# Turned tiles' transfers on SyncE, both far heads scaled by VectorE, and casts placed behind the weights' casts

## The chip, the cores and the metric

The kernel runs on one core of a Trainium2 chip. Its engines are TensorE (PE, matrix products), VectorE (DVE), ScalarE (ACT), GpSimd (POOL) and SyncE (SP, which here only issues transfers). The metric is device microseconds of one execution: 1052.34 us before the change, the median of 3 runs (1051.72 to 1052.66).

## What is computed

One layer of a hybrid encoder over 512 tokens of width 1024, in float32. From the normalised input h one combined projection feeds four mixers, whose outputs are gated and merged; a cross-attention into 256 memory tokens and a gated MLP follow. The change touches the two attentions among the mixers, and the preparation of the memory tokens:

```
# differential attention: 4 heads, two score maps each, chunk-causal
p = softmax(where(mask, q_c k_c^T * scale, -inf))       # c = 0, 1
out = (p[0] - lam * p[1]) v
# forgetting attention: 8 heads, frame-causal
c = cumsum(log_sigmoid(f_g + b_fgt))
s = q k^T * scale + c_q - c_k
out = softmax(where(mask, s, -inf)) v
# memory tokens, for the cross-attention
m = rms_norm(mem) ;  xk, xv = split(m @ w_xkv)
```

## The kernel before

**Precision.** Every operand of a large product is split into a high part (a cast to TensorE's fast float32) and a low part (the rest). A product takes three matmuls: high by high, high by low, low by high (`mm3`, L235 to L244).

**Weights.** A weight block of 512 KB is loaded by SP (`load_raw`, L164; the transfer's own line is L176) into one of two buffers `wr`. ACT casts it to `wh` (L192), then DVE subtracts for `wl` (L193). There are four buffers of each. `run_blocks` (L206) prepares blocks three jobs ahead of the one whose matmuls run. `last_weights` (L179) holds the last block's cast and subtraction.

**Background tasks.** Between the blocks, `Background` (L47) gives steps to generators: the attention of a head or of a pair of heads, and the memory tokens. A step has a planned cost and a wait before the next one. So the attention's small operations lie between weight blocks on every engine. The program then goes through a scheduler, which reorders the instructions of each engine by planned times. An edit of one instruction's engine therefore changes the order of others. `tc.issue_after(x)` holds an instruction behind instruction x in that order.

**PSUM.** Four kinds of tiles have two banks each: `ps_mm` (projections), `ps_av` (values), `ps_sc` (scores), `ps_tr` (transposes). A matmul into a bank waits until the reader of the tile that was there before is done. Readers of `ps_mm` are, by stage: ACT's copy and DVE's subtraction of a values block (`split`, L155 and L156), the same for queries and keys (L806 to L818), the tanh of a gate block on ACT (L1165), and DVE's merge of a branch (L1177). Readers of `ps_sc` are DVE's evacuations L929 (differential) and L1123 (forgetting), which add a mask or a bias and take a maximum.

**Attention.** `a_task` (L896) handles one head of the differential attention, `f_task` (L1055) a pair of heads of the forgetting attention. For each of the four query tiles of 128 rows (width w = 128 to 512 keys) the scores are made, evacuated, exponentiated on ACT (L934, L1129) and scaled. Then the probabilities must be turned, so that keys lie on partitions. There are two ways. *Near* heads (h = 3, and pairs 2 and 3) use TensorE's transposes (`to_keys_major`, L830). *Far* heads (h < 3, and pairs 0 and 1) turn squares of 32 by 32 on DVE (`turn_squares`, L845, recorded at L848), write the tile to DRAM (`put`, L850), read it back in another order into `ptl` (`get`, L859), then cast it in place on ACT to `pth` (L867) and subtract on DVE (L868). `values` multiplies these with v.

**Who issues, before.** `put` is issued by ACT. `get` is issued by ACT in `f_task`, held behind the last evacuation that `main` (L840) has noted, and by POOL in `a_task`. The casts of `split_in_place` (L863) are held behind that same noted evacuation. `mem_task` (L1291) turns two memory tiles in the same way, with its put on ACT and its get on POOL. In `f_task` each pair's first head is scaled by ACT (L1136) and the second by DVE (L1134). `GETS` and `SPLITS` (L893) say at which step a far head's tiles are read back and cast.

Of the kernel before, what the change touches and what calls it, by code (L numbers as in the profile page):

```python
# [17 lines left out]
F32 = mybir.dt.float32  # L18
# [7 lines left out]
P = 128  # L26
# [57 lines left out]
def hybrid_layer(ctx: ExitStack, tc: tile.TileContext, a: dict, out: bass.AP):  # L84
    nc = tc.nc
    V, A, G, PE, SP = nc.vector, nc.scalar, nc.gpsimd, nc.tensor, nc.sync
# [44 lines left out]
    for i in range(8):  # L131
        n = ("wh", "wl")[i % 2]
# [3 lines left out]
        elif i < 6:  # L136
            n = ("fz_raw", "fz", "fe", "fu", "fd")[i - 1]
# [41 lines left out]
    last_weights = []  # L179
# [200 lines left out]
    for i, plan in enumerate(plans):  # L380
        r_t = m1p.tile([P, P], F32, tag="fbias" if i == 2 else "ck", name=f"rows{i}", bufs=2)
        n = 0
# [19 lines left out]
    for t in range(2):  # L402
        y_t = m1p.tile([P, D], F32, tag="ptl", name="nt", bufs=2)
# [95 lines left out]
    for i in range(2):  # L499
        for p in range(3):  # L500
            first_half(i, p, w_g[i], glu[2:])
            if p == 2 - i:
                with tc.issue_after(casts[-1].ins):
                    y_t = normed(m1p, xs[:, 2 + i], gain, m1p.tile([P, D], F32, tag="ptl", name="nt", bufs=2), late)
# [345 lines left out]
    def put(e, w):  # L850
        d = dram.tile([2, P * S], F32, tag="turned", name="turned", bufs=6)[:e.shape[1], :P * w]
        d = d.rearrange("h (p x) -> p h x", p=P)
        A.dma_start(d, e[:, :, :w])
        return d

    def part_of(pt, n, local):
        return pt[:, local, :, :n].rearrange("p a t i -> p a (t i)")

    def get(d, n, pt, local, queue=A):  # L859
        with tc.issue_after(evacuations[0]) if queue is A else ExitStack():  # L860
            queue.dma_start(part_of(pt[1], n, local).bitcast(F32), d.rearrange("(a j) (b x) -> (j b) a x", j=32, b=4))  # L861

    def split_in_place(n, pt, local):  # L863
        hi, lo = (part_of(x, n, local) for x in pt)
        raw = lo.bitcast(F32)
        with tc.issue_after(evacuations[0]):
            A.copy(hi, raw)  # L867
        V.tensor_tensor(lo, raw, hi.bitcast(F32), ALU.subtract)  # L868

# [26 lines left out]
    def a_task(h, qk, v):  # L896
        es, pt, av = {}, None, None
        far = h < 3
        yield 0.0, 3.0
        for step in range(8 if far else 6):  # L900
            if step in ((5, 7) if far else (3, 5)):
                if av is None:
                    av = bank("av")
                vh, vl = (x[:, :, h * P:(h + 1) * P] for x in v[0])
                with tc.issue_after(steps_of[0]) if far else ExitStack():
                    values(av, lambda kt: ((vh[:, kt], 0), (vh[:, kt], 1), (vl[:, kt], 0)), pt,
                           step // 2 - (2 if far else 1))
            cost = 0.0
            if far:
                for qt in SPLITS.get(step, ()):  # L910
                    split_in_place(qt + 1, pt, qt % 2)
                    cost += 0.1 + 0.15 * qt
                for qt in GETS.get(step, ()):
                    if qt % 2 == 0:
                        pt = pt_tiles()
                    get(es.pop(qt)[:, 0], qt + 1, pt, qt % 2, G)
            elif 1 <= step <= 4:
                if step in (1, 3):
                    pt = pt_tiles()
                to_keys_major(es.pop(step - 1)[:, 0], step, pt, (step - 1) % 2)  # L920
                cost += 0.1 + 0.15 * step
            if step < 4:
                qt, w = step, (step + 1) * P
                e = es[qt] = e4()
                st = m1p.tile([P, 8], F32, tag="st8", name="st8", bufs=4)
                for c in range(2):
                    ps = bank("sc")
                    scores(ps, qk, c, qt * P, w)
                    V.tensor_tensor_reduce(e[:, c, :w], ps[:, :w], mask_a[:, S - w:], scale=1.0,  # L929
                                           scalar=-3.0e38, op0=ALU.add, op1=ALU.max,  # L930
                                           accum_out=st[:, c:c + 1])
                V.tensor_scalar(st[:, 2:4], st[:, 0:2], -HD ** -0.5, None, ALU.mult)
                for c in range(2):
                    A.activation(e[:, c, :w], e[:, c, :w], AF.Exp, bias=st[:, 2 + c:3 + c],  # L934
                                 scale=HD ** -0.5, accum_out=st[:, 4 + c:5 + c])
                V.reciprocal(st[:, 6:8], st[:, 4:6])
                V.tensor_scalar(st[:, 7:8], st[:, 7:8], lam, None, ALU.mult)
                A.activation(e[:, 1, :w], e[:, 1, :w], AF.Copy, scale=st[:, 7:8])
                V.scalar_tensor_tensor(e[:, 0, :w], e[:, 0, :w], st[:, 6:7], e[:, 1, :w], ALU.mult,
                                       ALU.subtract)  # L940
                cost += 0.6 + 0.0035 * w
                if far:
                    turn_squares(e[:, 1, :w], e[:, 0, :w])
                    es[qt] = put(e[:, 1:], w)
                    cost += 0.0015 * w
            if step == (7 if far else 5):
                e = e4()
                A.copy(e[:, 0], av)
            yield cost, (6.0 if step == 5 else 4.0) if far else 3.5

        ps = bank("tr")
        for t in range(NT):
            transpose(ps[:, t * P:(t + 1) * P], e[:, 0, t * P:(t + 1) * P])
        A.activation(e[:, 1], ps, AF.Square, scale=1.0 / math.sqrt(P))
        ms = m1p.tile([P, NT], F32, tag="ms4", name="ms4", bufs=2)
        V.tensor_reduce(ms, e[:, 1].rearrange("p (t c) -> p t c", t=NT), AX.X, ALU.add)
        r = rstd_of(m1p, [ms], NT)
        V.tensor_tensor(e[:, 0].rearrange("p (t c) -> p t c", t=NT),
                        ps.rearrange("p (t c) -> p t c", t=NT),
                        r.unsqueeze(2).to_broadcast([P, NT, P]), ALU.mult)  # L960
        yield 1.5, 3.5
        ps2 = bank("tr")
        for t in range(NT):
            transpose(ps2[:, t * P:(t + 1) * P], e[:, 0, t * P:(t + 1) * P])
        if "a" not in y:
            y["a"] = (y8b(), y8b())
        split(ps2, y["a"][0][:, h], y["a"][1][:, h], half["dn"])
        yield 0.6, 0.0
# [86 lines left out]
    def f_task(p, qk, v):  # L1055
# [19 lines left out]
        for step in range(8 if far else 6):  # L1075
# [33 lines left out]
            if step < 4:  # L1109
                qt, w = step, (step + 1) * P  # L1110
                e = es[qt] = e4()
                st = m1p.tile([P, 8], F32, tag="st8", name="st8", bufs=4)
                for j in range(2):
                    head = 2 * p + j
                    bias = m1p.tile([P, S], F32, tag="fbias", name="fbias", bufs=2)

                    G.tensor_scalar(bias[:, :w], ck[j][:, :w], -1.0, cq[:, qt, head:head + 1],  # L1117
                                    ALU.mult, ALU.add)
                    G.affine_select(out=bias[:, w - P:w], in_=bias[:, w - P:w], pattern=[[-1, P]],
                                    compare_op=ALU.is_ge, fill=BIG, base=0, channel_multiplier=1)  # L1120
                    ps = bank("sc")
                    scores(ps, qk, j, qt * P, w)
                    V.tensor_tensor_reduce(e[:, j, :w], ps[:, :w], bias[:, :w], scale=1.0,  # L1123
                                           scalar=-3.0e38, op0=ALU.add, op1=ALU.max,
                                           accum_out=st[:, j:j + 1])
                V.tensor_scalar(st[:, 2:4], st[:, 0:2], -HD ** -0.5, None, ALU.mult)
                turn_ready()
                for j in range(2):
                    A.activation(e[:, j, :w], e[:, j, :w], AF.Exp, bias=st[:, 2 + j:3 + j],  # L1129
                                 scale=HD ** -0.5, accum_out=st[:, 4 + j:5 + j])  # L1130
                V.reciprocal(st[:, 6:8], st[:, 4:6])
                for j in range(2):
                    if j:
                        V.tensor_scalar(e[:, j, :w], e[:, j, :w], st[:, 6 + j:7 + j], None, ALU.mult)  # L1134
                    else:
                        A.activation(e[:, j, :w], e[:, j, :w], AF.Copy, scale=st[:, 6 + j:7 + j])  # L1136
                cost += 0.6 + 0.0038 * w
                if far:
                    ready.append((qt, e, w))
                    cost += 0.003 * w  # L1140
# [150 lines left out]
    def mem_task():  # L1291
        for t in range(2):
# [8 lines left out]
                             y_t[:, i * S:(i + 1) * S])  # L1301
                yield 1.0, 0.0
            d = dram.tile([P * D], F32, tag="turned_m", name="turned_m", bufs=2)
            A.dma_start(d.rearrange("(p x) -> p x", p=P), m_t)
            G.dma_start(y_t.rearrange("p (a x) -> p a x", a=4), d.rearrange("(a j b x) -> (j b) a x", a=4, j=32, b=4))
            yield 0.0, 18.0
            hi, lo = (x[:, :, t * P:(t + 1) * P].rearrange("p k (a i) -> p k a i", a=4) for x in ns.mt)
            raw = y_t.rearrange("p (a k i) -> p k a i", a=4, i=32)
# [583 lines left out]
```

## Time and profile before

| | |
|---|---|
| median of 3 runs | 1052.34 us (1051.72 to 1052.66) |
| the profiled execution | 1052.56 us |
| its span in the trace | 1050.8 us, 14439 instructions |
| granted TensorE clock | 0.998 |
| DVE subtractions for `wl` (L193) | 140, 174.2 us |
| DMA | 163.85 MB, mean 156 GB/s |
| transfers issued on SP's queue | 38.0% of 16 engines' span |
| on ACT's queue | 8.9% |
| on POOL's queue | 3.7% |

A page of the profile shows one execution. Its first part gives busy time per engine, the second cuts the span into 40 slices of some 26 us and gives each engine's busy share in tenths (9 means 90% or more). Group lines read: line, engine, operation, output<-inputs by the program's names, shapes, count, total busy time, mean ns of one, and then the idle time of the engine just before them with what ended it. Timeline lines read: start, duration, engine, line, operation, and in brackets the idle time before it and its releaser. Lines that begin ACTq, POOLq or SPq are the issue of a transfer. Releasers are inferred.

### The profile page before, as it was taken

Reading aid. Unit: us, or ns where it says so; the run is one execution under the profiler, and the core shown is the slowest. Engines: PE = TensorE matmul, PEld = TensorE weight load, DVE = VectorE, ACT = ScalarE, POOL = GpSimd, SP = SyncE. Lnnn points to the kernel's source line nnn. Section 1 sums busy time; section 2 is a strip of 40 time slices with the busy share of each in tenths; the row PEclk is TensorE's granted clock in tenths of the full one; section 3 lists DMA queues with packets and bytes.
Section 4 is the critical chain, followed back from the end, with each engine's and each line's share of the span. In section 5 each row is a group of like instructions: output and inputs, shape, how many; then the busy total and the mean of one; then the engine's idle time right before and its main releaser. Section 6 shows DMA issues by size and latency. Waiting matters only on the chain.

```text
span 1050.8 us, 14439 instructions
## 1 busy us (share of the span) xinstructions
PE 1039.2 (99%) x5255; PEld 883.0 (84%) x5255; DVE 807.2 (77%) x1265; ACT 508.9 (48%) x838; POOL 157.7 (15%) x253
## 2 busy tenths in 40 slices
PE   9999999999999999999999999999999999999997
PEld 8888888888888988788888899999888888888886
DVE  7899998687777458776577898776767777667796
ACT  5322222376566355665434665655343333445662
POOL 4001000101210114422111031121112111111001
PEclk9999999999999999999999999999999999999999
DMA  7954333324433245652346834235676666725672
GB/s 249 316 164 104 103 99 100 101 83 124 134 104 111 60 120 172 182 149 82 100 154 230 277 121 124 78 101 182 194 246 221 220 223 219 220 81 181 214 216 80
DMA packets 175708, 163.85 MB, mean 156 GB/s; under 512 B 12543, under 2 KB 146924, under 8 KB 175637
## 3 DMA queue, kind: packets, MB, share of 16 engines
q1 hardware_dynamic: 152995, 119.91, 38.0%
q10 hardware_dynamic: 19122, 31.47, 8.9%
q0 software_dynamic: 3520, 11.56, 3.7%
q8 instruction: 41, 0.67, 0.3%
q14 instruction: 30, 0.25, 0.1%
HBM read 139.43 MB, written 23.48 MB: 155 GB/s over the span
## 4 chain that ended last, share of the span: by engine, by line
PE 90%; issue 4%; DVE 2%; ACT 1%; DMA 1%; POOL 1%; ACTq 0%; POOLq 0%; DVEq 0%
PE ps_mm L235 47%; PE ps_av L235 29%; PE ps_sc L235 7%; PE ps_tr L235 4%; PE ps_tr L241 2%; DMA ptl<-turned 1%; PE ps_mm L453 1%; PE ps_av L453 1%; POOL fbias L1117 0%; DMA xs<-in_x 0%; DVE qk L808 0%; ACT wh L192 0%; ACTq L861 0%; DVE e L1123 0%; DVE wl L193 0%
## 5 line engine op out<-in xcount | busy, mean ns | idle before, releaser
L192 ACT CAST wh<-wr 128x1024 fp32r<-128x1024 f32 (+1 forms) x140 | 146.7, 1048 | 258.9 <-PE ps_mm L235 156.9
L193 DVE TENSOR_TENSOR wl<-wr,wh 128x1024 fp32r<-128x1024 f32 (+1 forms) x140 | 174.2, 1245 | 86.3 <-ACT wh L192 86.0
L235 PE MATMUL ps_mm<-hth,wh 128*128 128x512 f32 (+1 forms) x616 | 230.8, 381 | 1.0 <-ACT wh L192 0.7
L235 PE MATMUL ps_mm<-hth,wl 128*128 128x512 f32 (+1 forms) x616 | 229.9, 379 | 0.0
L235 PE MATMUL ps_mm<-htl,wh 128*128 128x512 f32 (+1 forms) x616 | 229.8, 379 | 0.0
L235 PEld LDWEIGHTS ps_mm<-hth,wh 128*128 128x128 f32 x616 | 114.2, 188 | 22.5 <-ACT wh L192 1.1
L235 PEld LDWEIGHTS ps_mm<-hth,wl 128*128 128x128 f32 x616 | 114.0, 188 | 21.5
L235 PEld LDWEIGHTS ps_mm<-htl,wh 128*128 128x128 f32 x616 | 114.1, 188 | 20.4
L235 PE MATMUL ps_av<-htl,wh 128*128 128x512 f32 (+1 forms) x328 | 122.6, 374 | 0.0
L235 PE MATMUL ps_av<-hth,wh 128*128 128x512 f32 (+1 forms) x328 | 122.5, 373 | 0.0
L235 PE MATMUL ps_av<-hth,wl 128*128 128x512 f32 (+1 forms) x328 | 122.4, 373 | 0.0
L688 DVE SCALAR_TENSOR_TENSOR y<-y,par,y 128x508 f32<-128x508 f32 (+29 forms) x120 | 82.5, 726 | 0.1
L235 PEld LDWEIGHTS ps_av<-hth,wl 128*128 128x128 f32 x328 | 61.7, 188 | 10.9
L235 PEld LDWEIGHTS ps_av<-hth,wh 128*128 128x128 f32 x328 | 61.6, 188 | 10.9
L235 PEld LDWEIGHTS ps_av<-htl,wh 128*128 128x128 f32 x328 | 61.6, 188 | 10.8
L1683 DVE TENSOR_TENSOR wl<-dw,wh 128x1024 fp32r<-128x1024 f32 x32 | 40.0, 1256 | 15.5 <-ACT wh L1682 15.3
L1682 ACT CAST wh<-dw 128x1024 fp32r<-128x1024 f32 x32 | 33.4, 1051 | 22.6 <-PE ps_tr L235 8.1
L1117 POOL TENSOR_SCALAR fbias<-ck,cq 128x128 f32<-128x128 f32 (+3 forms) x32 | 28.3, 887 | 71.9 <-DVE st L1123 66.5
L1630 ACT ACTIVATE th<-c 128x512 f32<-128x512 f32 x22 | 13.9, 632 | 48.3 <-DVE c L615 48.3
L615 DVE SCALAR_TENSOR_TENSOR c<-ps_mm,par,c 128x510 f32<-128x510 f32 (+1 forms) x44 | 32.7, 744 | 0.7
L235 PE MATMUL ps_mm<-y8b,wh 128*128 128x512 f32 x96 | 30.6, 396 | 0.3 <-ACT ge L1165 0.3
L615 DVE SCALAR_TENSOR_TENSOR c<-ps_av,par,c 128x510 f32<-128x510 f32 (+1 forms) x40 | 29.8, 745 | 0.6
(486 smaller groups left out, 2103.5 us busy)
## 6 DMA issues: line engine op xcount, KB each, us to landing
wr<-in_w_up SPq DMA_DIRECT2D x44, 512.0 KB
wr<-in_w_in SPq DMA_DIRECT2D x38, 512.0 KB
wr<-in_w_gate SPq DMA_DIRECT2D x32, 512.0 KB
wp<-in_w_down ACTq DMA_DIRECT2D x22, 512.0 KB
sums<-wp ACTq DMA_DIRECT2D x22, 512.0 KB
dw<-sums SPq DMA_DIRECT2D x44, 256.0 KB
wr<-in_w_branch SPq DMA_DIRECT2D x16, 512.0 KB
wide<-in_w_out SPq DMA_DIRECT2D x12, 512.0 KB
```

Of the source, the lines that this page charges most:

```text
L192: last_weights[:] = [order(A.copy(hi, raw[:, :n])).ins, low.tensor_tensor(lo, raw[:, :n], hi.bitcast(F32), ALU.subtract).ins]
L193: low.tensor_tensor(lo, raw[:, :n], hi.bitcast(F32), ALU.subtract).ins]
L235: steps_of[:] = [PE.matmul(ps, lhs, rhs, start=start, stop=stop).ins]
L241: turns.append(PE.transpose(ps, x, ident[:n, :n]).ins)
L453: keep(PE.matmul(banks[c][:, :S // 2], w[p == 1][:, k, c * P:(c + 1) * P], ht[p == 2][:, i * 4 + k, :S // 2], start=(i, p, k) == (0, 0, 0) ...
L615: ins = V.scalar_tensor_tensor(dst[:, s:], src[:, :S - s], w(k), dst[:, s:], ALU.mult, ALU.add)
L688: ins = V.scalar_tensor_tensor(dst[:, s:], src[:, :S - s], pc("conv_dw", k * 4 + j), dst[:, s:], ALU.mult, ALU.add)
L1117: G.tensor_scalar(bias[:, :w], ck[j][:, :w], -1.0, cq[:, qt, head:head + 1], ALU.mult, ALU.add)
L1630: A.activation(th, c[:, 0], AF.Silu)
L1682: A.copy(hi, x)
L1683: V.tensor_tensor(lo, x, hi.bitcast(F32), ALU.subtract)
```

## The change

Five edits. `put` is issued by SP, not ACT. `get` is always issued by SP, with no hold behind an evacuation. In `a_task` the casts of turned tiles are held behind the cast of the last weight block, not behind the last noted evacuation; in `f_task` they stay where they were. In the far pairs of `f_task` both heads are scaled by DVE. In `mem_task` both transfers of the turned tiles are issued by SP. After the change lines beyond L865 have a number one lower.

```
     def put(e, w):
...
-        A.dma_start(d, e[:, :, :w])
+        SP.dma_start(d, e[:, :, :w])
...
-    def get(d, n, pt, local, queue=A):
-        with tc.issue_after(evacuations[0]) if queue is A else ExitStack():
-            queue.dma_start(part_of(pt[1], n, local).bitcast(F32), d.rearrange(...))
+    def get(d, n, pt, local):
+        SP.dma_start(part_of(pt[1], n, local).bitcast(F32), d.rearrange(...))
...
-    def split_in_place(n, pt, local):
+    def split_in_place(n, pt, local, after=evacuations):
...
-        with tc.issue_after(evacuations[0]):
+        with tc.issue_after(after[0]):
             A.copy(hi, raw)
...
                 for qt in SPLITS.get(step, ()):
-                    split_in_place(qt + 1, pt, qt % 2)
+                    split_in_place(qt + 1, pt, qt % 2, last_weights)
...
-                    get(es.pop(qt)[:, 0], qt + 1, pt, qt % 2, G)
+                    get(es.pop(qt)[:, 0], qt + 1, pt, qt % 2)
...
-                    if j:
+                    if j or far:
                         V.tensor_scalar(e[:, j, :w], e[:, j, :w], st[:, 6 + j:7 + j], None, ALU.mult)
...
-            A.dma_start(d.rearrange("(p x) -> p x", p=P), m_t)
-            G.dma_start(y_t.rearrange("p (a x) -> p a x", a=4), d.rearrange(...))
+            SP.dma_start(d.rearrange("(p x) -> p x", p=P), m_t)
+            SP.dma_start(y_t.rearrange("p (a x) -> p a x", a=4), d.rearrange(...))
```

More of the change, by code (lines that the diff above doesn't have):

```diff
@@ L857, in part_of @@
         return pt[:, local, :, :n].rearrange("p a t i -> p a (t i)")
-    def get(d, n, pt, local, queue=A):
-        with tc.issue_after(evacuations[0]) if queue is A else ExitStack():
-            queue.dma_start(part_of(pt[1], n, local).bitcast(F32), d.rearrange("(a j) (b x) -> (j b) a x", j=32, b=4))
-    def split_in_place(n, pt, local):
+    def get(d, n, pt, local):
+        SP.dma_start(part_of(pt[1], n, local).bitcast(F32), d.rearrange("(a j) (b x) -> (j b) a x", j=32, b=4))
+    def split_in_place(n, pt, local, after=evacuations):
         hi, lo = (part_of(x, n, local) for x in pt)
         raw = lo.bitcast(F32)
-        with tc.issue_after(evacuations[0]):
+        with tc.issue_after(after[0]):
             A.copy(hi, raw)
@@ L1303, in mem_task @@
             d = dram.tile([P * D], F32, tag="turned_m", name="turned_m", bufs=2)
-            A.dma_start(d.rearrange("(p x) -> p x", p=P), m_t)
-            G.dma_start(y_t.rearrange("p (a x) -> p a x", a=4), d.rearrange("(a j b x) -> (j b) a x", a=4, j=32, b=4))
+            SP.dma_start(d.rearrange("(p x) -> p x", p=P), m_t)
+            SP.dma_start(y_t.rearrange("p (a x) -> p a x", a=4), d.rearrange("(a j b x) -> (j b) a x", a=4, j=32, b=4))
             yield 0.0, 18.0
```

## Prediction, made before the result was known

> **What bounds the kernel now.** I read the page first: busy time per engine, then the forty slices.
>
> ```profile
> PE 1039.2 (99%) x5255; PEld 883.0 (84%) x5255; DVE 807.2 (77%) x1265; ACT 508.9 (48%) x838; POOL 157.7 (15%) x253
> ...
> PE   9999999999999999999999999999999999999997
> ...
> DVE  7899998687777458776577898776767777667796
> ...
> PEclk9999999999999999999999999999999999999999
> ```
>
> TensorE is busy in every slice at full clock. A change that touches no matmul can only remove its gaps, or add some. The table by stretches of 50 us says where the gaps are in the part that the change reaches (the two attention tasks, about 200 to 450 us):
>
> ```profile
> 250.00:300.00 50.00, 50.00 (x251) 42.31 (x250) 37.64 (x82) 29.71 (x58) 7.37 (x12) 1.00 0.40 118
> ...
> 350.00:400.00 50.00, 49.72 (x290) 43.30 (x290) 28.69 (x62) 27.69 (x49) 9.46 (x17) 1.00 0.35 98
> 400.00:450.00 50.00, 48.20 (x229) 39.80 (x228) 41.96 (x95) 29.83 (x67) 19.19 (x36) 1.00 0.65 179
> ```
>
> The columns are the length, then busy time of PE, PEld, DVE, ACT and POOL. PE lacks 1.80 us in 400 to 450 and 0.28 in 350 to 400. The table of TensorE's waits names them:
>
> ```profile
> PE ps_sc L235 <- DVE st L1123: 0.8, 1, 0.8
> ...
> PE ps_mm L235 <- ACT wh L192: 0.7, 1, 0.7
> PE ps_mm L235 <- ACT ge L1165: 0.3, 1, 0.3
> PE ps_mm L235 <- DVE qk L808: 0.2, 1, 0.2
> PE ps_tr L241 <- ACT e L948: 0.2, 1, 0.2
> ```
>
> The waits by starts of matmuls, from TensorE's timeline:
>
> ```profile
> 427.56 0.62 PE L235 MATMUL ps_sc<-qk 128*128 128x512 f32 x2
> 429.03 0.73 PE L235 MATMUL ps_sc<-qk 128*128 128x512 f32 x2 [0.85 <-DVE st L1123]
> 430.42 0.47 PE L235 MATMUL ps_mm<-hth,wh 128*128 128x512 f32 x1 [0.66 <-ACT wh L192]
> 430.73 0.40 PE L235 MATMUL ps_mm<-htl,wh 128*128 128x512 f32 x1
> 430.96 0.40 PE L235 MATMUL ps_mm<-hth,wl 128*128 128x512 f32 x1
> ```
>
> Consecutive 128x512 matmuls start 0.23 us apart (430.73 to 430.96). Two that start at 427.56 let the next start at 428.02; it came at 429.03, 1.01 late. The pair there lets the next start at 429.49; it came at 430.42, 0.93 late. Together **1.94 us**. The second has the weight's cast named as releaser, but that cast had ended 0.1 us earlier and belongs to another block; by the kernel's bank order it waited for the q/k subtraction (L818) that ended at 430.28. The tanh of L1165 costs 0.3 and the head-3 transpose (L948) 0.2. So **the most that the change can gain is some 2.5 us**, 0.24%. A difference under 0.2% (2.1 us) counts as no change, for about so much can be told from noise.
>
> **The change, part by part** (lines numbered as before the change).
>
> *Scaling on VectorE.* Eight far-pair scalings leave L1136 for L1134:
>
> ```profile
> L1136 ACT ACTIVATE e<-e,st 128x512 f32<-128x512 f32 x4 | 2.9, 727 | 3.5 <-issue 3.0 <-DVE st L1131 0.5
> L1134 DVE TENSOR_SCALAR e<-e,st 128x512 f32<-128x512 f32 x4 | 1.9, 487 | 0.1
> ```
>
> ACT loses at most 8 x 0.73 = 5.8 us, DVE gains at most 8 x 0.49 = 3.9. Neither is on the path by itself. But before the change the transposes waited for ACT's scaling, and at 427 the evacuation that released ps_sc stood behind those transposes. That link goes.
>
> *Transfers on SP.* ACT and POOL lose the issues, SP gains 52:
>
> ```profile
> 437.82 2.35 ACTq L861 DMA_DIRECT2D ptl<-turned  x4
> ...
> ptl<-turned POOLq DMA_DIRECT2D x3, 256.0 KB, 3.5
> ...
> L192 ACT CAST wh<-wr 128x1024 fp32r<-128x1024 f32 (+1 forms) x140 | 146.7, 1048 | 258.9 <-PE ps_mm L235 156.9
> ```
>
> Four gets held ACT's queue for 2.35 us. On SP, a put now waits for its transposes and a get for its put, and the next weights stand behind them. What hides this: 140 casts in the span's 1050.8 us are a weight every 7.5 us, and blocks are prepared three jobs ahead, so I estimate 15 to 22 us between a cast and its first matmul; in the whole span a cast is named once as TensorE's releaser. An issue (0.6 us each, 2.35 / 4) plus one landing (3.5) is well under that. Value: nothing. If the cover were gone, one late weight would cost the 4 us from load to cast (361.98 to 365.93, below). The mem task's two puts and gets come to the same, nothing, for they stand ahead of loads of the same slack.
>
> [...] No row here shows a far get on SP. [...]
>
> *Order of casts and evacuations.* The scheduler reorders both engines round these edits. I compared the order of instructions on each engine before and after. Where something moves ahead of an instruction that frees a PSUM bank that TensorE soon needs, I worked out a time from these rows. Five places matter.
>
> **At 262 us.** The order of scores and projections changes so that a ps_mm takes the bank freed by a q/k subtraction (L818), not by L1177:
>
> ```profile
> 259.47 1.18 DVE L193 TENSOR_TENSOR wl<-wr,wh 128x1024 fp32r<-128x1024 f32 x1
> 260.57 0.68 DVE L1177 SCALAR_TENSOR_TENSOR ge<-ge,ps_mm 128x512 f32<-128x512 f32 x1
> 261.17 1.39 DVE L818 TENSOR_TENSOR qk<-ps_mm,qk 64x512 fp32r<-64x512 f32 x2
> 262.58 0.56 DVE L929 CUSTOM_DVE_ANT_0 e<-ps_sc,mask_a 128x384 f32<-128x384 f32 x1
> 263.07 0.08 DVE L929 DVE_READ_ACCUMULATOR2_ANT st<- 128x1 f32 x1
> 263.07 0.55 DVE L868 TENSOR_TENSOR ptl<-ptl,pth 128x384 fp32r<-128x384 f32 x1
> ```
>
> That L818 now stands behind the low cast (ends at 260.6), an L868 (0.5) and an L929 (0.5): it begins at 261.6 and ends between 262.3 and 263.0, first or second of the pair; I take 262.7. TensorE wants the bank at about 261.8. Cost **+0.9**, bounds 0 and 1.3.
>
> **At 350 us** the values of head 3 are ready earlier; the listed 0.2 goes: **-0.2**, bounds 0 and -0.4.
>
> **At 366 us.** The clearest place:
>
> ```profile
> 361.98 1.50 SPq L176 DMA_DIRECT2D wr<-in_w_in  x2
> ...
> 364.69 0.37 ACT L155 CAST v<-ps_mm 128x256 fp32r<-128x256 f32 x1 [2.89 <-PE ps_mm L235]
> 365.10 0.43 DVE L156 TENSOR_TENSOR v<-ps_mm,v 128x256 fp32r<-128x256 f32 x1 [2.01 <-ACT v L155]
> 365.93 1.05 ACT L192 CAST wh<-wr 128x1024 fp32r<-128x1024 f32 x1 [0.86 <-DMA wr<-in_w_in]
> 366.29 0.40 PE L235 MATMUL ps_mm<-hth,wh 128*128 128x512 f32 x1
> 367.01 1.23 DVE L193 TENSOR_TENSOR wl<-wr,wh 128x1024 fp32r<-128x1024 f32 x1 [1.48 <-ACT wh L192]
> ```
>
> The matmul at 366.29 reuses the bank of the v block that ACT copies at 364.69 and DVE subtracts at 365.10. After the change ACT's cast of the weight (365.93) and DVE's low part (367.01) stand ahead of this copy and subtraction. The cast can't begin before the landing at 365.93. So the chain is: cast to 366.98, low part to 368.24, then subtraction 0.43, to 368.67. TensorE, which wants the bank at 366.29, waits 2.4 us; if the weight lands a little earlier, less. Cost **+2.1**, bounds 0 (landing before 363.6) and 2.5. It is queue order, so nothing hides it: engines ahead of it idle for 2.89 and 2.01 us now.
>
> **At 411 us** the L1177 that frees a bank moves behind a low cast and four L868:
>
> ```profile
> 411.86 0.68 DVE L1177 SCALAR_TENSOR_TENSOR ge<-ge,ps_mm 128x512 f32<-128x512 f32 x1
> 412.56 1.23 DVE L193 TENSOR_TENSOR wl<-wr,wh 128x1024 fp32r<-128x1024 f32 x1
> ```
>
> Between 0 (TensorE comes later than the DVE work) and 1.5 (the low cast's 1.23 and one small L868); I take **+0.5**, nearer nothing since DVE has gaps here.
>
> **427 to 430 us.** The scores of 429.03 move behind 3.6 us more of matmuls, and the q/k subtraction ahead of the transposes. Of 1.94 some 0.25 stays: **-1.7**, bounds -1.94 and -0.8.
>
> **At 441 us.** Now the tanh (L1165) that frees the bank is on ACT behind two exponentials, a copy and a cast, and the exponentials wait on DVE behind a pair of transposes:
>
> ```profile
> 435.66 1.67 DVE L848 STREAM_TRANSPOSE e<-e 128x384 f32<-128x384 f32 x2
> 435.73 0.71 ACT L1129 ACTIVATE e<-e,st 128x512 f32<-128x512 f32 x1
> 440.85 0.67 ACT L1165 ACTIVATE ge<-ps_mm,s_b_gate 128x512 f32<-128x512 f32 x1
> ```
>
> From the evacuated scores to the tanh's end: transposes 1.67, the small row operation some 0.2, exponentials 2 x 0.71, copy some 0.6 (a 64x512 of ACT), cast 1.05, tanh 0.67: 5.6 us. TensorE has 28 matmuls of 0.23, 6.4 us, between these scores and the bank. That leaves 0.8 us for the evacuation, and DVE has a low cast (1.23) and scalings (up to 0.49 each) ahead of it. Without backlog nothing is lost; with all of it, 5.6 + 0.8 + 2.7 - 6.4 = 2.7. I take 1.5, and subtract the 0.3 to 0.5 that the wait costs now: **+1.1**, bounds -0.4 and +2.3.
>
> The sum: +0.9 - 0.2 + 2.1 + 0.5 - 1.7 + 1.1 = **+2.7 us** on the profiled execution's 1052.56, 1055.3; that execution is 0.2 over the median, 1052.34, so **1055.0**.
>
> **The rivals.**
>
> *Faster.* The waits that the profile lists go, and none takes their place: -1.94 - 0.3 - 0.2, 1049.9. It decides at two points: the weight of 366 must land before 363.6, 2.3 us earlier than now (SP would have to issue it as much earlier), and DVE's backlog at 441 must stay under 0.8 us. For it: ACT loses work and waits. Against it: SP only gains work, and the cast stands in the wrong order whatever ACT has free.
>
> *No change.* TensorE waits at 366, but by a part only, or the bank order at 262 and 411 turns out covered: -2.2 + 2.1 to 2.7, 1051.5 to 1054. [...]
>
> *Weights late.* A put on SP waits longer than the cover and a load behind it is late: 4 us each, so 1059 for one with the rest as forecast. Against it: 15 us of cover; the waits list has no such entry.
>
> **How the numbers follow.** Chances: the forecast with its bounds 0.50, no change 0.33, faster 0.10, weights late 0.07. Slower by over 0.2% means above 1054.4: the forecast's larger part (0.46) and late weights, 0.53; faster means below 1050.2: 0.10; within: 0.37. The forecast's own range is 1053 to 1057.5, from the bounds of 366 and 441 that don't all fall one way. To leave out no more than 2 in 10 the range goes down over the no-change case to 1051 and up to 1057.6.
>
> **What would show it.** A TensorE gap of about 2 us at 366, ended by L156 behind the low cast (step 366 right), or none (wrong). No gap at 427 to 430 (right). A gap ended by L1165 near 443 and one ended by L818 at 262. If SP's queue is what ACT's casts wait for, longer than now, and TensorE for the casts, the cover was less than estimated. The forecast is wrong if the reordered instructions in fact run at times at which their inputs are ready anyway.

## The result, and the profile after the change

The changed kernel took **1058.12 us**, the median of 4 runs (1056.37 to 1060.30), against 1052.03 before: a ratio of 1.0059, with a 95% interval of 1.0047 to 1.0071. The forecast was 1055.0, with a range up to 1057.6. The sign was right; the loss was 6.1 us where 2.7 was forecast. A second measurement, beside other kernels and told below, gave 1056.23 against 1051.40: 1.0049, 1.0032 to 1.0066. That spread is part of the explanation.

The profiled execution took 1060.3 us with a span of 1058.5 us, 7.7 more than before. From its page:

```profile
PE 1043.3 (99%) x5255; PEld 885.1 (84%) x5255; DVE 810.7 (77%) x1273; ACT 504.3 (48%) x830; POOL 145.5 (14%) x239
```

ACT and POOL have less to do, DVE 3.5 us more, as the diff says. TensorE is busy 4.1 us longer with the same number of matmuls. So some matmuls became slower, and that no step of the forecast had. The stretches of 50 us (length; busy PE, PEld, DVE, ACT, POOL; granted clock; DMA share; GB/s) show both where TensorE is idle and where its clock is low:

```profile
250.00:300.00 50.00, 47.68 (x233) 39.45 (x232) 34.80 (x74) 26.28 (x52) 3.30 (x6) 1.00 0.42 123
...
350.00:400.00 50.00, 48.20 (x290) 42.59 (x290) 26.50 (x58) 24.35 (x41) 9.25 (x18) 0.97 0.31 88
400.00:450.00 50.00, 48.33 (x226) 40.36 (x225) 42.44 (x95) 27.12 (x60) 18.07 (x34) 0.97 0.64 173
```

Idle: 2.32 us in 250 to 300 (before: none), 1.80 in 350 to 400, 1.67 in 400 to 450 (before: 1.80, elsewhere in it). The clock is 0.97 in the last two; it was 1.00. TensorE's waits:

```profile
PE ps_mm L235 <- DVE v L156: 1.8, 1, 1.8
PE ps_mm L235 <- ACT ge L1164: 1.7, 1, 1.7
PE ps_mm L235 <- DVE ge L1176: 1.7, 1, 1.7
PE ps_mm L394 <- DVE e L344: 1.3, 1, 1.3
PE ps_mm L235 <- DVE qk L818: 0.7, 1, 0.7
```

(L394 is the start of the program and was there before.) Four new waits, 5.9 us; of the old ones the 0.8, 0.7, 0.3 of 427 to 442 and the 0.2 at 350 are gone, 2.0 us. That is +3.9. The rest is the clock: the next rows, of the same view, are the two stretches behind the last two gaps in time.

```profile
372.00:375.00 3.00, 3.00 (x10) 2.28 (x9) 1.94 (x7) 1.34 (x2) 0.00 (x0) 0.53 0.66 192
447.00:452.00 5.00, 4.97 (x15) 3.94 (x16) 5.00 (x9) 2.05 (x6) 0.00 (x0) 0.66 0.38 132
```

In each TensorE is granted half its clock for 3.4 us (in the same view the clock is 0.50 from 372.20 to 375.62 and from 447.30 to 450.71): 5 us at 0.66 lose 0.34 x 5, 1.7 us of full clock. The text calls such a stretch a fall. In TensorE's timeline one sees the first begin 1.1 us after the gap at 369 to 371, when starts go from 0.23 to 0.42 us apart (the second, at 447.3, begins 0.3 us after its gap):

```profile
371.07 0.50 PE L235 MATMUL ps_mm<-hth,wh 128*128 128x512 f32 x1 [1.80 <-DVE v L156]
371.40 0.39 PE L235 MATMUL ps_mm<-htl,wh 128*128 128x512 f32 x1
...
372.43 0.63 PE L235 MATMUL ps_mm<-hth,wl 128*128 128x512 f32 x1
372.85 0.63 PE L235 MATMUL ps_mm<-hth,wh 128*128 128x512 f32 x1
```

Two such falls are 3.4 us. Waits and falls make 7.3 of the 7.7 us. The third gap, of 1.7 us at 285 to 287, brought no fall: the clock is 1.00 from 285 to 292.

The gap at 366 (here 369) is the one that was forecast, cause for cause. In ACT's timeline the cast comes after 3.75 us of idle time, ended by its weight's landing, with the v copies behind it; in DVE's (the second rows) the low part stands ahead of the subtraction in the same way:

```profile
368.38 1.05 ACT L192 CAST wh<-wr 128x1024 fp32r<-128x1024 f32 x1 [3.75 <-DMA wr<-in_w_in]
369.33 0.36 ACT L155 CAST v<-ps_mm 128x256 fp32r<-128x256 f32 x1
```

```profile
369.45 1.23 DVE L193 TENSOR_TENSOR wl<-wr,wh 128x1024 fp32r<-128x1024 f32 x1 [3.57 <-ACT wh L192]
370.60 0.42 DVE L156 TENSOR_TENSOR v<-ps_mm,v 128x256 fp32r<-128x256 f32 x1
```

The gap at 285 to 287 was not forecast. In DVE's timeline the subtraction of the last turned tile (L867) stands ahead of the merge L1176, whose bank TensorE waits for; in ACT's (the second rows) the cast before that subtraction waits for the tile:

```profile
286.15 0.69 DVE L867 TENSOR_TENSOR ptl<-ptl,pth 128x512 fp32r<-128x512 f32 x1 [4.26 <-ACT pth L866]
286.76 0.68 DVE L1176 SCALAR_TENSOR_TENSOR ge<-ge,ps_mm 128x512 f32<-128x512 f32 x1
```

```profile
285.50 0.62 ACT L866 CAST pth<-ptl 128x512 fp32r<-128x512 f32 x1 [4.45 <-DMA ptl<-turned]
```

Before the change that merge stood ahead of the subtraction. The tile itself was no earlier then: read back by POOL, it let ACT's cast begin at 285.43 us. What changed is the order. DVE's timeline of before, and ACT's (the second rows):

```profile
281.71 0.68 DVE L1177 SCALAR_TENSOR_TENSOR ge<-ge,ps_mm 128x512 f32<-128x512 f32 x1
...
286.08 0.69 DVE L868 TENSOR_TENSOR ptl<-ptl,pth 128x512 fp32r<-128x512 f32 x1 [2.00 <-ACT pth L867]
```

```profile
285.43 0.62 ACT L867 CAST pth<-ptl 128x512 fp32r<-128x512 f32 x1 [4.47 <-DMA ptl<-turned]
```

### The profile page after: what moved, and what is told of

Read it like the earlier page. It is cut to its first block, busy times and chain, and to the rows that moved or that the text cites. A ratio compares the mean times of both kernels' runs of the same rounds, so it can differ in the third digit from the quotient of the medians.

```text
span 1058.5 us, 14460 instructions
## 1 busy us (share of the span) xinstructions
PE 1043.3 (99%) x5255; PEld 885.1 (84%) x5255; DVE 810.7 (77%) x1273; ACT 504.3 (48%) x830; POOL 145.5 (14%) x239
## 4 chain that ended last, share of the span: by engine, by line
PE 87%; DMA 4%; DVE 4%; ACT 2%; issue 2%; SPq 0%; DVEq 0%; POOL 0%; POOLq 0%; ACTq 0%
PE ps_mm L235 47%; PE ps_av L235 29%; PE ps_sc L235 6%; PE ps_tr L235 2%; PE ps_tr L241 2%; DMA dw<-sums 1%; DMA ptl<-turned 1%; PE ps_mm L453 1%; ACT wh L192 1%; PE ps_av L453 1%; DMA turned<-e 0%; DMA dw<-in_w_down 0%; DMA xs<-in_x 0%; DVE wl L193 0%; DVE wl L1682 0%
## 5 line engine op out<-in xcount | busy, mean ns | idle before, releaser
L235 PE MATMUL ps_mm<-y,wh 128*128 128x512 f32 x96 | 30.7, 395 | 0.7 <-DVE qk L818 0.7
```

What stands on the lines that cost most here:

```text
L235: steps_of[:] = [PE.matmul(ps, lhs, rhs, start=start, stop=stop).ins]
```

## The experiments

**The theory** after the result: time is lost only where the new order of an engine puts an instruction that still waits for data ahead of one that frees a PSUM bank; the order comes from the edits together, and a gap on TensorE can bring a stretch at half clock, as those of 1.8 and 1.7 us did with 3.4 us each. **Rivals:** SP's fuller queue makes loads or turned tiles late (queue theory); DVE's eight added scalings delay what is behind them (backlog theory). Differences are given to "before" as measured beside each run.

### One part of the change alone, or one left out

Edits 1, 2 and 5 alone (from the kernel before; `put` as in the diff):

```
-            queue.dma_start(part_of(...))         # f_task: ACT, held
+            (SP if queue is A else queue).dma_start(part_of(...))   # not held
-                    get(es.pop(qt)[:, 0], qt + 1, pt, qt % 2, G)
+                    get(es.pop(qt)[:, 0], qt + 1, pt, qt % 2, SP)
```

> Only the transfers (all puts and gets, the memory tokens' too) go to SP; scaling and holds as before the change. Order theory (the time is lost where an engine's order of instructions puts a waiting one ahead of one that frees a PSUM bank): in this kernel's order the cast of the weight at 366 us stands behind the v copies as before, the merges at 285 us stand ahead of the 512-wide subtraction, and the scores of 429 us stay where they were, so none of the four new gaps comes; within 1 us of before, 1051 to 1053. Queue theory (SP's queue with 52 more transfers makes weights or turned tiles late): most of the loss is here, 1055 to 1058, with TensorE waiting for weights' casts.

Measured: 1051.81 us against 1051.83, ratio 0.9999 (0.9989 to 1.0008). With all 52 transfers on SP nothing is lost. TensorE's waits name no weight's cast. The queue theory falls, as far as it makes the transfers alone the cause.

Edit 3 alone (the hold of the casts in `a_task`, with `split_in_place` as in the diff):

```
-                    split_in_place(qt + 1, pt, qt % 2)
+                    split_in_place(qt + 1, pt, qt % 2, last_weights)
```

> Only the far heads' casts of the differential attention are held behind the last weight's cast. Order theory: the PSUM bank order at 262 us changes as in the changed kernel and costs 0.8 to 1.0 us there; nothing at 285, 366 or 441; 1053, between 1052.3 and 1054. Queue theory: nothing, 1052.

Measured: 1052.62 against 1051.83, 1.0008 (0.9999 to 1.0017). Its trace has the gap at 262, ended by L818 after 0.7 us, and otherwise the gaps of before. The place is as expected; the difference in time is too small to be told from none.

All but edit 3, which is undone by that line alone:

> The change without the new hold of the casts (transfers on SP, both far heads scaled by VectorE). Order theory: no gap at 262, 285 or 366; the gap of 427 to 430 goes (1.9 us), the one at 441 to 447 comes (1.3 to 1.8 more than now, and up to 1.7 more where TensorE's clock falls after it); 1051 to 1054. Queue theory: the whole loss stays, 1056 to 1058. Backlog theory (VectorE's added scalings delay everything behind them): the whole loss stays, 1055 to 1058.

Measured: 1052.00 against 1051.83, 1.0005 (0.9996 to 1.0015). No gap at 262, 285 or 366; those of 427 to 430 shrank to 0.2, the tanh of L1165 took 1.0. The loss is away, so backlog alone doesn't make it. (A wait of 1.1 us near 1029 us, far behind the part that the change reaches, is in this execution too.)

All but edit 4 (scaling):

```
-                    if j or far:
+                    if j:
```

> The change without the moved scaling. TensorE's order is the same as in the changed kernel. Order theory: gaps at 262 (0.8), 285 (1.8) and 366 (1.9) stay, the one at 441 too or smaller; 1054.5 to 1058, up to two falls of the clock of 1.7 each among it. Backlog theory: back to before, 1052 to 1053.

Measured: 1055.32 against 1051.83, 1.0031 (1.0019 to 1.0043). Gaps at 262 (0.7) and 366 (1.7) stay, the tanh's is 0.7. The loss is 3.5 us, where the whole change, measured beside other runs, lost 4.8 and 6.1; the scaling has a part at 441 (below). At 285 there was no wait, though the subtraction stands ahead of the merge there too, since the tile landed sooner; ACT's timeline of this kernel:

```profile
282.82 0.62 ACT L867 CAST pth<-ptl 128x512 fp32r<-128x512 f32 x1 [1.81 <-DMA ptl<-turned]
```

SP's timeline of this kernel, and then of the changed one, has the get and the weight behind it (the shift of the line numbers by one begins at `get`: L861 before the change, L860 after it):

```profile
280.16 0.36 SPq L861 DMA_DIRECT2D ptl<-turned  x1
280.81 0.37 SPq L176 DMA_DIRECT2D wr<-in_w_branch  x1
```

```profile
280.59 0.36 SPq L860 DMA_DIRECT2D ptl<-turned  x1
281.05 0.46 SPq L176 DMA_DIRECT2D wr<-in_w_branch  x1
```

From issue to cast it took 2.7 us in one and 4.9 in the other. In the second the two transfers are issued closer together, 0.46 us against 0.65. That doesn't decide it: with the transfers alone and without edit 3 the two are 0.45 and 0.46 us apart, and it took 3.4 and 3.1 us. Read back by POOL, before the change, it took 4.9 too (280.53 and 285.43). What sets the time of landing is open. It sets the size of this gap.

So neither the transfers nor the hold loses much alone: the orders that make the gaps at 285 and 366 need both. The hold was then split by head, with the rest of the change as it is:

```
-                    split_in_place(qt + 1, pt, qt % 2, last_weights)
+                    split_in_place(qt + 1, pt, qt % 2, last_weights if h == 0 else evacuations)
```

> The changed kernel with the new hold of the casts for head 0 of the differential attention alone (heads 1 and 2 hold behind the last noted evacuation, as before the change). Order theory: this hold alone makes the orders at 262 us and 285 us; 0.8 lost at 262, 0 to 2 at 285 by the landing of one get, none at 366; the gap at 441 as without the new holds. 1052.8 to 1055, nearest 1053.5. Rival (the hold costs by casts that come late themselves, wherever they stand): heads 0 and 2 share the loss evenly, 1054 each.

Measured: 1054.99 against 1051.89, 1.0030 (1.0019 to 1.0041). Gaps at 262 (0.7) and 285 (0.8), none at 366; the tanh's is 0.9. The time is at the upper end of what was expected.

> The changed kernel with the new hold for head 2 alone. Order theory: it alone puts the weight's cast ahead of the v copies at 366 us; 1.9 us lost there, and in part of the executions a fall of TensorE's clock behind it of 1.7 more; no gap at 262 and 285. 1053.5 to 1056, nearest 1054.5. Rival as for head 0: 1054 for both, and no single gap of 1.8 us.

Measured (`h == 2`): 1054.99 against 1051.89, 1.0029 (1.0019 to 1.0039). A gap at 366 (1.8), none at 262 and 285; the tanh's is 1.7. The times are the same, as the rival had it, but the gaps are at separate places, as the theory had it. Its nine executions already hint at the clock: the four at a mean granted clock of 0.999 took 1053.6 to 1054.7 us, the two at 0.997 took 1055.0 and 1055.5, the two at 0.996 1055.6 and 1056.1, the one at 0.995 1057.4.

### The order at 441 us

Two trials to get the tanh ahead of the casts held every weight's cast on ACT behind the last noted evacuation, the first in the kernel with edits 1, 2 and 5, the second in the one without edit 3:

```
+        with tc.issue_after(evacuations[0]) if evacuations else ExitStack():
+            cast = order(A.copy(hi, raw[:, :n])).ins
```

> Transfers on SP alone, and every weight's cast on ScalarE held behind the last noted evacuation, so that the tanh of a gate block stands ahead of casts. If the gaps are a matter of order, the ones of 427 to 442 (together 2.4 us) get smaller and the time falls below before, 1050 to 1051.5. If holding the casts makes weights late, slower, 1053 or more, with TensorE waiting for casts.

> The change without the new hold of the far casts, and with every weight's cast held behind the last noted evacuation. The tanh at 441 us then stands ahead of the cast: of the 1.1 us gap there about 1 us goes; 1050 to 1051.5. If holding the casts makes weights late, 1053 or more.

Measured: 1056.98 (1.0048, 1.0032 to 1.0065) and 1058.47 (1.0065, 1.0050 to 1.0080). Both slower, and not by late casts, which no wait names: the hold moved other instructions, and new waits for bank readers came (2.1 us for L821's q/k subtraction in one, 2.3 for the tanh and 1.9 for a scores' evacuation in the other, by these kernels' line numbers). The granted clock was lower too: 0.996 to 0.997 in the first's four executions and 0.995 to 0.996 in the second's, where before has 0.997 to 0.999 beside them. A miss: a rule for all casts does more than the one exchange that was wanted. So one exchange was made, in the changed kernel (the block's subtraction on DVE is held with its cast):

```
+        with tc.issue_after(evacuations[0]) if hi.tensor.name.startswith('wh_4064') else ExitStack():
             last_weights[:] = [order(A.copy(hi, raw[:, :n])).ins, ...
```

> The changed kernel with one weight block's cast (the one ahead of the tanh at 441 to 447 us) held behind that tanh; TensorE's and SP's orders stay the same, and ScalarE's first difference is these two instructions changing places. Order theory: the gap there (1.7) shrinks by up to the cast's 1.05 us, to 0.7, and the falls of the clock behind it with it: 1 to 2.5 us less than the change, 1055.5 to 1057. Rival (the time there is VectorE's backlog of scalings, or SP's queue): the gap stays at 1.7, 1058.

Measured: 1054.67 against 1051.40; the changed kernel beside it 1056.23. ACT's timeline of the changed kernel:

```profile
445.21 1.05 ACT L192 CAST wh<-wr 128x1024 fp32r<-128x1024 f32 x1
446.29 0.69 ACT L1164 ACTIVATE ge<-ps_mm,s_b_gate 128x512 f32<-128x512 f32 x1
```

ACT's timeline with the exchange:

```profile
442.60 0.69 ACT L1164 ACTIVATE ge<-ps_mm,s_b_gate 128x512 f32<-128x512 f32 x1
443.19 1.04 ACT L192 CAST wh<-wr 128x1024 fp32r<-128x1024 f32 x1
```

TensorE's wait for the tanh went from 1.7 to 0.7 us, about the cast's 1.05, and the time fell by 1.6, of which the wait is 1.0. That the order of these two instructions costs 1.0 us of the wait is shown. It is not the only cause: in the kernel without the scaling the cast still stands ahead of the tanh (440.57 and 441.65 us in its ACT timeline), and there too the wait is 0.7. So the added scaling on DVE and the cast's place both have a part, and taking away either leaves 0.7. The hold of edit 3 has one too: without it, with the cast ahead of the tanh and the scaling added, the wait was 1.0.

> The same one swap in the kernel without the new hold of the far casts. Order theory: its gap of 1.1 near 439 us goes almost, 1050.8 to 1051.5, so 0.5 to 1 us below before. Rival: unchanged, 1052.

Measured, the same exchange in the kernel without edit 3: 1050.91 against 1051.40, 0.9996 (0.9986 to 1.0005). TensorE's only waits between 200 and 630 us are the 0.2 each at 220 and 350. It has the lowest median here, and is no different from the kernel before by its interval. The listed waits that it removes are 2.0 us; that removing them gains as much is not shown, 0.5 us was measured. Its table of stretches has TensorE busy without a gap in 400 to 450:

```profile
400.00:450.00 50.00, 50.00 (x241) 41.74 (x240) 45.51 (x100) 27.61 (x60) 21.10 (x35) 1.00 0.65 181
```

### The clock

> The changed kernel once more, beside the others on one chip, for the spread of its executions. Clock theory: its executions lie in steps of some 1.7 us by the number of falls of TensorE's clock, 1055.5 to 1060.5, and the higher the time the lower the mean granted clock (0.999 with none, 0.995 with two to three). Rival: the spread has nothing to do with the clock.

Measured: 1056.23 (1055.75 to 1057.50) against 1051.40, clocks 0.998, 0.997, 0.997, 0.998. With the first four runs: 1060.30 at 0.995; 1058.29 and 1057.96 at 0.997; 1056.37 at 0.999. In the profiled execution of this measurement the same four gaps are there (1.7, 1.7, 0.7 and, at 285, 0.6), and the clock is 1.00 in 350 to 400 and in 400 to 450; behind the first of them in its table of stretches:

```profile
372.00:375.00 3.00, 3.00 (x15) 2.48 (x14) 1.46 (x7) 1.74 (x3) 0.00 (x0) 1.00 0.76 219
```

15 matmuls in these 3 us, where the first profile had 10. Its span is 1054.4 us: without a fall 3.6 over the profiled execution of before, against 7.7 with two. (Over the median span of the executions of before beside it, 1049.6, it is 4.8. Its waits, 4.7 us less the 2.0 that went, make 2.7; the rest is as large as the scatter between executions and is not explained.) So here a fall is a matter of the execution. The steps are not as clean as expected: two executions at 0.997 took 1056.3 and 1057.5. The mean clock can't count falls to one: it varies from 0.998 to 0.999 in the executions of before too, and one fall, 1.7 us lost in some 1055, is 0.0016. Part of what the mean lacks to 1 is no loss either: 3.7 us in the profile of before and 3.6 in the first of the changed kernel are at clock 0.50 at the very end of the span, behind the last matmul.

To measure a gap's price by itself, nine gaps were put into the up-projection of the kernel before. In the first attempt ACT rewrote part of a block's high weights with their own value, behind its first reading of the previous block's sums:

```
+                if n > 7 and n % 4 == 0:
+                    flat = hi.rearrange("p k c -> p (k c)")
+                    for w in [1024]:          # [64], [1024], [1024, 1024]
+                        with tc.issue_after(st["first"]):
+                            A.copy(flat[:, :w], flat[:, :w].bitcast(F32))
```

> The kernel before, with nine gaps put into the up-projection (about 700 to 900 us): at every fourth block ScalarE rewrites 64 columns of the block's high weights with their own value, behind its reading of the previous block's sums, so that TensorE waits. Estimated gap 1.1 us each (an activation of about 0.65, a small copy, hand-overs). Clock theory (an idle stretch of TensorE near 2 us can be followed by some 3.3 us at half clock, which costs 1.7 more): too short, so the loss is 9 times the gap alone, some 10 us: 1062. Rival (the falls of the clock in the changed kernel had another cause): the loss is 9 gaps in all three of these kernels.

> As the one with short gaps, but 1024 columns are rewritten: gaps of about 2.0 us. Clock theory: in about half of the nine a fall to half clock of some 3.3 us follows, so the loss is 9 x 2.0 + 4 to 5 x 1.7, 26 us: 1078, and mean granted clock near 0.992. Rival: 18 us, 1070, clock as before.

> As the one with short gaps, but 1024 columns are rewritten twice: gaps of about 3.0 us. Clock theory: a fall behind nearly every gap: 9 x 3.0 + 9 x 1.7 = 42 us, 1094, granted clock near 0.985. Rival: 27 us, 1079, clock as before.

Measured: 1051.40, 1051.07 and 1051.46 against 1051.11. No gap came: the scheduler put another block's matmuls ahead of the one that waited. In the second attempt each block's matmuls are held behind the previous block's:

```
+                    with tc.issue_after(steps_of[0]):
                         channel_major(ps, (hi, lo), ns.hf)
```

> As the one with middle gaps in order, but only 64 columns are rewritten: gaps of about 1.1 us. Clock theory: too short for a fall, the loss is the nine gaps alone, 10 us: 1062, clock as before. Rival (any gap can bring a fall): more than the nine gaps, and a lower clock.

> The kernel before, with nine gaps in the up-projection: at every fourth block ScalarE rewrites 1024 columns of the block's high weights with their own value, behind its reading of the previous block's sums, and each block's matmuls are held behind the previous block's, so that TensorE can't go on with another block. Gaps of about 2.0 us. Clock theory: in part of the nine a fall to half clock of some 3.3 us follows, so the loss is 9 x 2.0 plus 3 to 6 times 1.7, 23 to 28 us: 1075 to 1080, clock near 0.99. Rival: 18 us, 1070, clock as before.

> As the one with middle gaps in order, but 1024 columns are rewritten twice: gaps of about 3.0 us. Clock theory: a fall behind nearly every gap: 9 x 3.0 plus 9 x 1.7, 42 us: 1094, clock near 0.985. Rival: 27 us, 1079, clock as before.

The gaps came out longer than estimated. From the tables of TensorE's waits of the three kernels, short, middle and long (total, times, longest):

```profile
PE ps_mm L235 <- ACT wh L1644: 15.5, 9, 1.7
```

```profile
PE ps_mm L235 <- ACT wh L1644: 22.7, 9, 2.5
```

```profile
PE ps_mm L235 <- ACT wh L1644: 34.3, 9, 4.6
```

Times: 1070.49 against 1052.41 (+18.1, clock 0.997 and 0.998), 1081.99 against 1051.40 (+30.6, clock 0.993 and 0.994), 1103.54 against 1052.41 (+51.1, clock 0.982 to 0.985). Over their waits of 15.5, 22.7 and 34.3 us that is 2.6, 7.9 and 16.8. The stretches behind the gaps tell why. With short gaps all nine have clock 1.00; the first of them in the table of stretches:

```profile
745.00:750.00 5.00, 4.50 (x20) 3.74 (x21) 2.99 (x4) 0.44 (x2) 1.70 (x3) 1.00 0.91 297
```

With middle gaps four of the nine have a fall, among them the first but not the second:

```profile
743.00:748.00 5.00, 4.68 (x13) 3.69 (x14) 2.02 (x3) 0.27 (x1) 2.19 (x3) 0.66 0.69 215
769.00:774.00 5.00, 4.50 (x20) 3.74 (x21) 2.19 (x4) 0.44 (x1) 2.21 (x3) 1.00 0.82 277
```

With long gaps all nine have one; the first:

```profile
745.00:750.00 5.00, 4.99 (x15) 3.95 (x16) 0.69 (x1) 0.00 (x0) 2.19 (x3) 0.66 0.43 118
```

With 0.15 us more per gap between starts (with short gaps 2.11 us apart, for a wait of 1.72 and the usual 0.23), four falls of 1.7 in the middle kernel give 22.7 + 1.4 + 6.8 = 30.9, nine in the long one 34.3 + 1.4 + 15.3 = 51.0: both within 0.3 us of the measured. That close is in part luck, since executions of these kernels spread by 2 to 4 us. In the short kernel 1.2 of the 2.6 us stay unexplained, and what the hold on the matmuls costs without a rewriting was not run. That a gap brings falls, that their share rises with its length (none of nine at 1.7 us, four of nine at 2.5, nine of nine at 3.8 on the mean), and the price of each are shown.

What decides which of several equal gaps brings a fall is not shown. The nine of the middle kernel are all 2.5 us long (22.7 us in total, 2.5 the longest), and five brought none; in the changed kernel the same two gaps, at 366 and 441, brought a fall each in the first profile (1.8 and 1.7 us) and none in the second (1.7 each).

## Why the prediction was right or wrong

**The bound and the sign** were right: TensorE has no slack, and only its gaps matter. That 2.5 us could be gained was an upper bound; the kernel with the exchange and without edit 3 has these waits away and measured 0.5 us below before, within its interval.

**Scaling and transfers on SP at nothing**: right for the transfers alone, 1051.81. The scaling by itself was not run; with the transfers, and without the hold, it makes 1052.00, and within the whole change it adds to the wait at 441. TensorE never waited for a weight's cast there, so the cover was never used up.

**262 us, +0.9**: right; 0.7 of wait, ended by L818.

**350 us, -0.2**: right; the 0.2 is gone.

**366 us, +2.1**: right in place, chain and size; 1.8 of wait in one profile, 1.7 in the other. But the step stopped at the end of the gap. In the first profile a fall followed it, 1.7 us.

**411 us, +0.5**: too high, though its bounds began at 0. No wait came there. The same kind of wait, L1176 behind a subtraction of a turned tile, came at 285 instead.

**427 to 430 us, -1.7**: right; both waits of it are gone.

**441 us, +1.1**: right in mechanism; the wait is 1.7, so +1.4 over the 0.3 of before. The cast ahead of the tanh and DVE's scalings, which the forecast's chain has, each have a part in it: with one of them away it is 0.7.

**The steps that failed** are two, and both are terms that the sum left out.

The list of "five places" was one short. At 285 the subtraction of the 512-wide turned tile had passed ahead of the merge L1176 on DVE, and I missed it, while its tile was ready only 4.9 us after the issue in the first profile: 1.7 us of wait there, 0.6 in the second. And each gap was priced at its own length. The clock behind a gap had no term, that is, it was put at nothing: in the first profile two falls, 3.4 us, stood behind the gaps at 366 and 441, in the second none.

Put right, the gaps give -2.0 + 0.7 + 1.8 + 1.7 + 1.7 = 3.9 us for the first profile and -2.0 + 0.7 + 1.7 + 1.7 + 0.6 = 2.7 for the second. That the latter is the forecast's 2.7 is luck: mainly, the 0.5 that didn't come at 411 stands against the 0.6 at 285. With two falls the first is 7.3, of the 7.7 measured; the first runs' median of 6.1 lies between none and two falls. The second measurement's 4.8 is 2.1 more than its waits, and that part is open.

The range was also narrower than the forecast's own bounds: with all of them at their upper end the sum is 1.3 + 0 + 2.5 + 1.5 - 0.8 + 2.3 = +6.8, which is 1059.1; the range stopped at 1057.6.

**The rivals.** "Faster" fell at both points that it named: the weight at 366 landed 0.9 us ahead of TensorE's wish for the bank (368.4 and 369.3), where 2.7 were needed, and the tanh came late. "Weights late" had no support. "No change" is what the transfers alone and the hold alone measured; it was argued from partly covered gaps in the whole change, which was not what happened.

## What to carry to other kernels

Where one engine is full and a scheduler orders the rest, edits that are free by themselves (here the transfers and the hold) can cost together, since the new orders have new heads of queue: look, on every engine, for an instruction that waits on a transfer and stands ahead of the reader that frees a bank. Price a gap on TensorE by its length, and by 1.7 us more for each fall that can follow it: here four of nine placed gaps of 2.5 us brought one, all nine of 3.8 on the mean, and none of nine of 1.7. Hold one instruction, not a class of them: the single exchange gained 1.6 us in the changed kernel, the rule for all casts lost 5 to 7 against the kernels that it was put into.

## What the runs showed of the hardware that was not expected

A gap of 2.5 us on TensorE brought 3.4 us at half clock in four of nine cases, and gaps of 3.8 us on the mean (the longest 4.6) in nine of nine. Gaps of 1.7 and 1.8 us brought it in two of the changed kernel's three in its first profile, and in none of fourteen others: nine placed ones, and five in the profiles of the changed kernel's second measurement (1.7 twice), of the one with the hold for head 2 (1.8 and 1.7) and of the one without the scaling (1.7). The matmuls behind a gap ran on at full clock for a while before the fall, 1.1 us in one case and 0.3 in another.

The same 256 KB read back from DRAM, issued by SP 0.45, 0.46, 0.46 and 0.65 us ahead of a weight of 512 KB, was there for its cast 3.4, 3.1, 4.9 and 2.7 us after its issue, not in the order of these distances.
